# The opening in another order on four engines, and another place for T4's products, in a hybrid encoder kernel

## The chip, the core and the metric

The kernel runs on one core of one Trainium2 chip. The metric is the device time of one execution in microseconds (us), here as the median of several runs. The core's engines run side by side, each through a program of its own, in order: PE (TensorE: matrix products and transpositions; the load of its stationary operand is listed as PEld), DVE (VectorE), ACT (ScalarE) and POOL (GpSimd). SP (SyncE) issues most of the transfers. An engine that needs something of another waits for it, and everything behind it in its program waits as well.

## The reference

The input x of [1, 1024, 1024] float32, with 16 learned rows in front of it, runs through one layer. All is kept in float32 accuracy; the kernel gets it by splitting each float32 operand into a high and a low part and adding three products: high by high (hh), high by low (hl), low by high (lh).

```python
h = rmsnorm(h_res, norm1_w)                 # x * rsqrt(mean(x*x) + 1e-6) * w
proj = h @ w_in                             # q k v z beta a | sc_b sc_c sc_x | gate_a gate_b
o_dn = gated_deltanet_bidir(q, k, v, z, b_raw, a_raw, conv_w, A_log, dt_bias, dn_norm_w)
y_a = o_dn @ w_branch_dn
y_b = (sc_b * depthwise_conv_centred(sc_c * sc_x, sc_conv_w)) @ w_branch_sc
merged = sigmoid(gate_a) * y_a + sigmoid(gate_b) * y_b
h_res = h_res + merged @ w_out
h2 = rmsnorm(h_res, norm2_w)
gu = h2 @ w_gate_up
h_res = h_res + (silu(gu[..., :D_FF]) * gu[..., D_FF:]) @ w_down
out = rmsnorm(h_res, final_norm_w)[:, 16:]
```

## The kernel before

The program goes through stages: the opening (norm of nine row tiles of x, transposition, first products), the combined projection with the DeltaNet scans between its products, the merge gates, the two branch projections, the output projection, and the feed-forward part. In the opening and in the stage behind it, the order of PE, DVE and ACT is the order in which the code is written.

The opening works on tiles of 128 rows of h. Tile t is loaded into xs[t] (xr in the profile; tile 0 is the 16 learned rows and 112 rows of x). `square(t)` on ACT takes the sum of squares into ss and then its root; `normed(t)` on DVE takes a reciprocal, one Newton step on it (`inv_root`), and multiplies the tile by ss and by the row of norm weights, w1row. `turn(t, ...)` transposes the tile on PE by eight 128x128 transpositions into two PSUM banks, g = 0 for the first 512 columns and g = 1 for the rest. `high(t, g)` on ACT casts a bank into hTh (the high part), and `lows(t, g)` on DVE takes the low part (the tiles al). `weights(u)` splits the first weight tile of a unit u: ACT casts into wh, POOL subtracts into wl, each in two halves of four of the eight blocks k. `steps(gen0, KT, order)` then lets PE make the 24 products of a unit over 336 columns (bank pm, line 328), in an order of the three kinds hh, lh, hl. Behind them come the products `ba(0)` (lines 1125 and 1126), tile 3, and unit 1's products.

The norm weights reach all 128 partitions like this: w1one holds them as one row of 1024 on one partition, loaded third on SP's queue; PE multiplies a column of ones by it, 512 at a time, and DVE copies the two banks into w1row. `idle_turns(n)` makes n transpositions of the identity that nobody reads. The taps of the short convolutions are loaded as rows and turned by two transpositions, which ACT scales into wc and cols.

The loads of the opening are issued by SP in the order of the code. They take eight completion semaphores in turn, so the ninth load waits until the first has landed, and so on.

The last gate pair is made by `last_pair`. Its products are made by a scheme with seven block products instead of eight: A11 and so on are split weight tiles, B11, B12, B21 and B22 the four blocks of h transposed (tiles hTh and al), and S1 to S4 and T1 to T4 sums of blocks. `product(bank, a, b)` issues 12 products of 128x512 (line 1430). T4's product adds to the bank (pd) that holds S2 by T2 and S3 by T3. B11's product goes to a bank po (pe), ACT copies it to o1 (line 1598), and then B21's product adds to the same bank, so it must wait for that copy. Behind the pair the first branch projection starts (lines 134 to 136), over px: rows of p_d that ACT casts and DVE subtracts (lines 101 and 102) while the pair is made. This last part lies outside the stretches with a fixed order; a scheduler of the framework places its instructions on each engine.

## Time and profile before

| what | us |
|---|---|
| median of three runs | 1985.89 |
| lowest and highest of them | 1984.41, 1986.49 |
| the profiled execution, as a run | 1983.87 |
| its span, from the first to the last instruction | 1982.2 |
| PE busy within the span | 1966.1 |
| start of the first product of line 328 | 17.02 |
| start of the first product of line 134 | 1074.57 |

The prediction shows rows of several views. In the timeline and in the chain of waits a row begins with its start and its length in us from the start of the span; then come the engine, the line, the operation and the tiles, and in brackets how long the engine stood idle before it and what released it. A row of the waits gives the engine, what it waited for, the us in total, how often, and the longest. PE's rows in the timeline overlap: products are pipelined, and the length of one reaches to its modelled end, so the pace is read from the starts.

### The profile page before, as it was taken

Reading aid. Unit: us, or ns where it says so; the run is one execution under the profiler, and the core shown is the slowest. Engines: PE = TensorE matmul, PEld = TensorE weight load, DVE = VectorE, ACT = ScalarE, POOL = GpSimd, SP = SyncE. Lnnn points to the kernel's source line nnn. Section 1 sums busy time; section 2 is a strip of 40 time slices with the busy share of each in tenths; the row PEclk is TensorE's granted clock in tenths of the full one; section 3 lists DMA queues with packets and bytes.
Section 4 is the critical chain, followed back from the end, with each engine's and each line's share of the span. In section 5 each row is a group of like instructions: output and inputs, shape, how many; then the busy total and the mean of one; then the engine's idle time right before and its main releaser. Section 6 shows DMA issues by size and latency. Waiting matters only on the chain.

```text
span 1982.2 us, 31846 instructions
## 1 busy us (share of the span) xinstructions
PE 1966.1 (99%) x11999; PEld 1718.1 (87%) x11999; DVE 1396.6 (70%) x3015; ACT 839.1 (42%) x1968; POOL 107.7 (5%) x407
## 2 busy tenths in 40 slices
PE   9999999999999999999999999999999999999998
PEld 8999999999999999888888888888887888888887
DVE  6888688888888888844954544469676766646575
ACT  6472354636464646344444221225332333324344
POOL 2011101010101010100000000000000000000000
PEclk9999999999999999999999999999999999999999
DMA  3122222212122212222236743123366754477654
GB/s 134 66 90 75 61 86 60 76 60 76 59 76 60 76 59 76 70 86 95 97 128 240 247 157 99 64 85 111 123 224 235 250 186 167 170 274 245 192 172 169
DMA packets 124689, 251.52 MB, mean 127 GB/s; under 512 B 44981, under 2 KB 46438, under 8 KB 122103
## 3 DMA queue, kind: packets, MB, share of 16 engines
q1 hardware_dynamic: 123959, 248.44, 37.6%
q8 instruction: 94, 1.54, 0.3%
q10 hardware_dynamic: 576, 1.05, 0.1%
q14 instruction: 60, 0.49, 0.1%
HBM read 181.20 MB, written 68.25 MB: 126 GB/s over the span
## 4 chain that ended last, share of the span: by engine, by line
PE 92%; DVE 4%; DMA 3%; ACT 1%; issue 1%; SPq 0%; DVEq 0%; ACTq 0%
PE pm L328 31%; PE pd L1430 12%; PE pe L1430 6%; PE pm L1430 4%; PE pe L136 2%; PE pe L134 2%; PE pe L135 2%; PE pd L890 1%; PE pd L869 1%; PE pd L853 1%; PE pd L856 1%; PE pe L2040 1%; PE pe L2041 1%; PE pe L2039 1%; PE pd L886 1%; PE pe L590 1%
## 5 line engine op out<-in xcount | busy, mean ns | idle before, releaser
L328 PE MATMUL pm<-hTh,wh 128*128 128x320 f32 (+4 forms) x1248 | 428.4, 349 | 0.4 <-ACT hTh L1090 0.2
L328 PE MATMUL pm<-al,wh 128*128 128x320 f32 (+4 forms) x1248 | 427.7, 348 | 0.0
L328 PE MATMUL pm<-hTh,wl 128*128 128x320 f32 (+4 forms) x1248 | 425.9, 347 | 0.0
L328 PEld LDWEIGHTS pm<-hTh,wh 128*128 128x128 f32 x1248 | 233.9, 189 | 11.9 <-issue 1.3
L328 PEld LDWEIGHTS pm<-hTh,wl 128*128 128x128 f32 x1248 | 234.2, 189 | 10.2 <-issue 0.4
L328 PEld LDWEIGHTS pm<-al,wh 128*128 128x128 f32 x1248 | 234.1, 189 | 9.7
L102 DVE TENSOR_TENSOR al<-raw,ring_h 128x1024 fp32r<-128x1024 f32 x73 | 88.6, 1223 | 65.0 <-ACT ring_h L101 64.3
L101 ACT CAST ring_h<-raw 128x1024 fp32r<-128x1024 f32 x73 | 76.7, 1053 | 107.0 <-PE pd L2041 40.2
L350 DVE SCALAR_TENSOR_TENSOR kq<-ra,wc,kq 128x520 f32<-128x520 f32 x128 | 96.5, 754 | 4.9 <-ACT kq L380 4.0
L977 DVE TENSOR_TENSOR wl<-raw,wh 128x512 fp32r<-128x512 f32 x112 | 76.0, 689 | 31.1 <-ACT wh L980 30.4
L876 ACT ACTIVATE w<-pd,small 128x128 f32<-128x128 f32 x128 | 39.8, 363 | 125.0 <-PE pd L869 124.3
L487 DVE TENSOR_TENSOR fP<-fP,tm 128x135 f32<-128x135 f32 (+23 forms) x248 | 71.6, 289 | 5.1
L483 DVE TENSOR_TENSOR tm<-fP,fN 128x135 f32<-128x135 f32 (+23 forms) x248 | 71.8, 290 | 4.4
L980 ACT CAST wh<-raw 128x512 fp32r<-128x512 f32 x112 | 66.2, 621 | 3.7 <-issue 3.6
L101 ACT CAST wh<-raw 128x1024 fp32r<-128x1024 f32 x37 | 38.8, 1050 | 52.9 <-PE pm L135 16.6
L1978 ACT ACTIVATE b<-b 128x512 f32<-128x512 f32 x20 | 12.6, 632 | 103.6 <-DVE b L1396 103.6
L843 ACT ACTIVATE jk<-NP 128x128 f32<-128x128 f32 x64 | 19.9, 311 | 76.5 <-DVE NP L839 75.5
L102 DVE TENSOR_TENSOR wl<-raw,wh 128x1024 fp32r<-128x1024 f32 x37 | 45.1, 1220 | 10.0 <-ACT wh L101 9.9
L1430 PE MATMUL pd<-b_hl,wh 128*128 128x512 f32 x168 | 51.9, 390 | 0.0
L863 DVE SCALAR_TENSOR_TENSOR r<-pd,negEG,vS 128x128 f32<-128x128 f32 x120 | 36.7, 344 | 20.8 <-PE pd L853 20.4
L899 DVE SCALAR_TENSOR_TENSOR S<-S,eGl,pd 128x128 f32<-128x128 f32 x104 | 31.5, 340 | 28.1 <-PE pd L886 28.0
L1396 DVE TENSOR_TENSOR b<-pd,b 128x512 f32<-128x512 f32 x21 | 14.5, 689 | 51.9 <-PE pd L1430 51.9
(626 smaller groups left out, 4793.8 us busy)
## 6 DMA issues: line engine op xcount, KB each, us to landing
raw<-in_w_in_dram SPq DMA_DIRECT2D x72, 512.0 KB
raw<-in_w_gate_up_dram SPq DMA_DIRECT2D x44, 512.0 KB
sums<-in_w_down_dram SPq DMA_DIRECT2D x22, 512.0 KB
t_d<-sums SPq DMA_DIRECT2D x11, 1024.0 KB
raw<-s_d SPq DMA_DIRECT2D x44, 256.0 KB
raw<-t_d SPq DMA_DIRECT2D x44, 256.0 KB
act_d<-b SPq DMA_DIRECT2D x43, 256.0 KB
raw<-act_d SPq DMA_DIRECT2D x33, 256.0 KB
```

What stands on the lines that cost most here:

```text
L101: nc.scalar.copy(hi, src)
L102: nc.vector.tensor_tensor(out=lo, in0=src, in1=hi.bitcast(F32), op=ALU.subtract)
L134: mm(po[:m, :n], wh[:, k, :m], xhk[:, t0:t0 + n], start=(k == 0), stop=False)
L135: mm(po[:m, :n], wh[:, k, :m], xlk[:, t0:t0 + n], start=False, stop=False)
L328: mm(po[:, :n], ww[:, k], f(k)[:, t0:t0 + n], start=i == 0, stop=i == 3 * KT - 1)
L350: nc.vector.scalar_tensor_tensor(out=acc, in0=raw[:, h0 + t:h0 + t + hn], scalar=wc[:, t, col:col + 1], in1=acc, op0=ALU.mult, op1=ALU.add)
L483: nc.vector.tensor_tensor(out=tv, in0=fP[:, 0:r, j:j + 1].broadcast_to([P, r, n]), in1=fN[:, j:j + 1, j + 1:32].broadcast_to([P, r, n]), o ...
L487: nc.vector.tensor_tensor(out=fP[:, 0:r, j + 1:32], in0=fP[:, 0:r, j + 1:32], in1=tv, op=ALU.subtract)
L876: nc.scalar.activation(w[d], b2[:, 2 + d], AF.Copy, scale=ce[:, c, d:d + 1])
L977: nc.vector.tensor_tensor(out=u[1][1][:, k], in0=u[2][:, k], in1=u[1][0][:, k].bitcast(F32), op=ALU.subtract)
L980: nc.scalar.copy(u[1][0][:, k], u[2][:, k])
L1430: mm(po, x[:, k], at(y, k), start=i == 0 and not add_to, stop=i == 11, skip_group_check=add_to)
```

## The change

The norm weights come as eight rows of 128 (w1rows), by a load that ACT issues ahead of its table load. PE transposes them into eight columns (w1cols), DVE copies these, and PE transposes each column, broadcast to 128 columns, so that the bank holds the weights on all partitions; DVE copies the two banks into w1row as before. The idle turns become 8, 2, 12 and 2 instead of 8, 20, 4 and 4. The third tile is multiplied in two halves of 512 columns. The taps' transpositions move ahead of the third tile's and go into one bank. ACT casts the first half of the weights ahead of all transposed tiles, and then goes by halves of the columns: the first halves of the three tiles, with the second half of the weights between them, then the second halves. DVE takes the lows in the same order. A new tiny copy on POOL, from the last column of the third tile, writes into wl before the subtractions do. PE makes unit 0's hh and lh products of the first four blocks, then those of the other four, and then hl. In `last_pair`, T4's product moves behind B11's.

On PE the opening reads as follows, up to the first unit's products (pd, pe and pm are banks, ident the identity). First the program before, then the changed one:

```order
L98 MATMUL pd_185<-ident 128x128 x8
L1136 MATMUL pm_194<-w1one,ones_151 128x512
L1136 MATMUL pm_197<-w1one,ones_151 128x512
L98 MATMUL pd_227<-ident 128x128 x20
L98 MATMUL pe_248<-ident,xr_153 128x128 x4
L98 MATMUL pe_253<-ident,xr_153 128x128 x4
L98 MATMUL pd_264<-ident 128x128 x4
L98 MATMUL pd_269<-ident,xr_154 128x128 x4
```

```order
L98 MATMUL pd_184<-ident 128x128 x8
L98 MATMUL pm_193<-ident,w1rows 128x8
L98 MATMUL pd_196<-ident 128x128 x2
L98 MATMUL pm_199<-ident,w1cols 128x128 x4
L98 MATMUL pm_205<-ident,w1cols 128x128 x4
L98 MATMUL pd_239<-ident 128x128 x12
L98 MATMUL pe_252<-ident,xr_153 128x128 x4
L98 MATMUL pe_257<-ident,xr_153 128x128 x4
L98 MATMUL pd_262<-ident 128x128 x2
L98 MATMUL pd_265<-ident,xr_154 128x128 x4
```

The two products from w1one are gone, nine transpositions and two idle turns stand in their place, and the twenty idle turns ahead of the first tile have become twelve.

On ACT the stretch from the third tile's root to the last transposed tile reads as follows, before and changed (jk and ss belong to the squares, raw to the weights):

```order
L1070 ACTIVATE ss_218<-ss_218,eps 128x1
L1090 CAST hTh<-pe_248 128x4x128
L1090 CAST hTh<-pe_253 128x4x128
L1104 CAST wh_181<-raw_167 128x512 x2
L1090 CAST hTh<-pd_269 128x4x128
L1090 CAST hTh<-pd_274 128x4x128
L1090 CAST hTh<-pd_284 128x4x128
L1090 CAST hTh<-pe_289 128x4x128
```

```order
L1069 ACTIVATE ss_229<-ss_229,eps 128x1
L1105 CAST wh_180<-raw_166 128x512
L1091 CAST hTh<-pe_252 128x4x128
L1091 CAST hTh<-pd_265 128x4x128
L1105 CAST wh_180<-raw_166 128x512
L1091 CAST hTh<-pd_278 128x4x128
L1091 CAST hTh<-pe_257 128x4x128
L1091 CAST hTh<-pd_270 128x4x128
L1091 CAST hTh<-pe_283 128x4x128
```

The weights' first half has moved to the front, and the three first halves of the tiles (pe_252, pd_265, pd_278) stand ahead of the second ones.

On PE the last gate pair reads as follows around T4's products (pd from b and w), with B11's products ahead of them in the changed program; first before, then changed:

```order
L1430 MATMUL pm_12916<-b_2064_12135,mB_12908 128x512 x8
L1430 MATMUL pd_12915<-b_2108_12466,w_2087_12254 128x512 x12
L1430 MATMUL pe_12968<-hTh,wh_12898 128x512
L1430 MATMUL pe_12968<-al_124,wh_12898 128x512
L1430 MATMUL pe_12968<-hTh,wl_12899 128x512
```

```order
L1441 MATMUL pe_12953<-hTh,wh_12895 128x512
L1441 MATMUL pe_12953<-al_124,wh_12895 128x512
L1441 MATMUL pe_12953<-hTh,wl_12896 128x512
L1441 MATMUL pd_12912<-b_2108_12463,w_2087_12251 128x512 x12
L1441 MATMUL pe_12953<-hTh,wh_12895 128x512
L1441 MATMUL pe_12953<-al_125,wh_12895 128x512
L1441 MATMUL pe_12953<-hTh,wl_12896 128x512
```

T4's twelve products stand between B11's (hTh, al_124) and B21's (hTh, al_125). The scheduler also moved four of B22's products, which stood between B11's and B21's, behind them, and three additions of DVE ahead of pieces of px. Elsewhere the order on the engines is the same in both programs.

The diff, cut to its core:

```diff
@@ -322,7 +322,7 @@
         (wh, wl), (xh, xl) = w, xx
         t0 += C0
         parts = {"hh": (wh, lambda k: xh[:, k]), "hl": (wh, lambda k: xl[k]), "lh": (wl, lambda k: xh[:, k])}
-        seq = [(m, k) for m in sweep for k in range(KT)] if sweep else [(m, k) for k in range(KT) for m in ("hh", "hl", "lh")]
+        seq = [(m, k) for m, kk in sweep for k in kk] if sweep else [(m, k) for k in range(KT) for m in ("hh", "hl", "lh")]
         for i, (m, k) in enumerate(seq):
             ww, f = parts[m]
             mm(po[:, :n], ww[:, k], f(k)[:, t0:t0 + n], start=i == 0, stop=i == 3 * KT - 1)
@@ -1026,24 +1026,23 @@
         eps = st.tile([P, 1], F32, name="eps")
         nc.gpsimd.memset(warm, 1.0)
         nc.gpsimd.memset(eps, EPS)
-        nc.scalar.activation(warm, warm, AF.Sqrt)
         baT = d1.tile([P, L], F32, tag="vT", name="baT", bufs=2)[:64]
         wba = st.tile([P, KT, 64], F32R, name="wba")
         raw = st.tile([P, KT, 32], F32, name="wba_raw")
         rows = st.tile([P, 2, P], F32, name="rows")
         wc = c1.tile([P, 5, 24], F32, name="wc")
         size = lambda t: P if t < 8 else META
-        w1one = st.tile([1, D], F32, name="w1one")
-        ones1 = st.tile([1, P], F32, name="ones1")
-        nc.gpsimd.memset(ones1, 1.0)
-
+        w1rows = st.tile([KT, P], F32, name="w1rows")
+        w1cols = st.tile([P, KT], F32, name="w1cols")
+        nc.scalar.dma_start(w1rows, norm1_w.rearrange("o (k p) -> (o k) p", p=P))
+
+        nc.scalar.activation(warm, warm, AF.Sqrt)
         xs = [st.tile([P, D], F32, tag="xr", name=uid("xr"), bufs=9) for _ in range(9)]
         units = []
         for t, xr in enumerate(xs):
             if t == 0:
                 nc.sync.dma_start(xr[:META], meta)
                 nc.sync.dma_start(xr[META:P], x[0:P - META])
-                nc.sync.dma_start(w1one, norm1_w[0:1, :])
             else:
                 nc.sync.dma_start(xr[:size(t)], x[P * t - META:P * t - META + size(t)])
             if t == 2:
@@ -1069,18 +1068,20 @@
             nc.scalar.activation(jk[:p], xs[t][:p], AF.Square, accum_out=ss[:, 0:1])
             nc.scalar.activation(ss[:, 1:2], ss[:, 0:1], AF.Sqrt, scale=1.0 / D, bias=eps[:p])
 
-        def normed(t):
+        def normed(t, pieces=1):
 
             p, ss = size(t), scale[t]
             inv_root(ss)
-            nc.vector.scalar_tensor_tensor(out=xs[t][:p], in0=xs[t][:p], scalar=ss[:, 2:3], in1=w1row[:p],
-                                           op0=ALU.mult, op1=ALU.mult)
+            for i in range(pieces):
+                c = slice(D // pieces * i, D // pieces * (i + 1))
+                nc.vector.scalar_tensor_tensor(out=xs[t][:p, c], in0=xs[t][:p, c], scalar=ss[:, 2:3], in1=w1row[:p, c],
+                                               op0=ALU.mult, op1=ALU.mult)
 
         banks = {}
 
-        def turn(t, *make):
+        def turn(t, *make, gs=(0, 1)):
             p = size(t)
-            for g in range(2):
+            for g in gs:
                 pt = banks[t, g] = make[g]().rearrange("p (k t) -> p k t", k=4)
                 for k in range(4):
                     transpose(pt[:, k, :p], xs[t][:p, (4 * g + k) * P:(4 * g + k + 1) * P], p)
@@ -1097,9 +1098,9 @@
                 nc.vector.tensor_tensor(out=l_[:, :, c], in0=banks[t, g][:, k, :p],
                                         in1=hx[0][:, 4 * g + 2 * i:4 * g + 2 * i + l_.shape[1], c].bitcast(F32), op=ALU.subtract)
 
-        def weights(u):
-
-            for i in range(2):
+        def weights(u, parts=(0, 1)):
+
+            for i in parts:
                 k = slice(4 * i, 4 * i + 4)
                 nc.scalar.copy(u[1][0][:, k], u[2][:, k])
                 nc.gpsimd.tensor_tensor(out=u[1][1][:, k], in0=u[2][:, k], in1=u[1][0][:, k].bitcast(F32), op=ALU.subtract)
@@ -1128,37 +1129,47 @@
                     f()
             return lambda: nc.scalar.copy(baT[:, t0:t0 + n], po[:64, :n])
 
-        first, second = ("hh", "lh", "hl"), ("hh", "hl", "lh")
+        whole, halves = range(KT), (range(4), range(4, KT))
+        first, second = (tuple((m, whole) for m in ms) for ms in (("hh", "lh", "hl"), ("hh", "hl", "lh")))
+        opening = (*((m, kk) for kk in halves for m in ("hh", "lh")), ("hl", whole))
 
         idle_turns(8)
+        pw = psm()
+        transpose(pw[:, :KT], w1rows, KT)
+        nc.vector.tensor_copy(w1cols, pw[:, :KT])
+        idle_turns(2)
         for i in range(2):
             pw = psm()
-            mm(pw, ones1, w1one[:, 512 * i:512 * i + 512], start=True, stop=True)
+            for k in range(4):
+                transpose(pw[:, k * P:(k + 1) * P], w1cols[:, 4 * i + k:4 * i + k + 1].broadcast_to([P, P]))
             nc.vector.tensor_copy(w1row[:, 512 * i:512 * i + 512], pw)
         for t in range(3):
             square(t)
-            normed(t)
-        idle_turns(20)
+            normed(t, 1 + (t == 2))
+        idle_turns(12)
         turn(0, psd, psd)
+        idle_turns(2)
+        turn(1, pss, pss)
+        taps = psm()
+        transpose(taps[:, :120], rows[:120, 0], 120)
+        transpose(taps[:, 128:153], rows[:25, 1], 25)
+        turn(2, pss, psd, gs=(0,))
+        turn(2, pss, psd, gs=(1,))
+        nc.gpsimd.tensor_copy(u0[1][1][:, 0, 0:1], xs[2][:, D - 1:D])
+        weights(u0, (0,))
         high(0, 0)
-        high(0, 1)
-        weights(u0)
-        idle_turns(4)
-        turn(1, pss, pss)
-        idle_turns(4)
-        turn(2, pss, psd)
-        for t in (1, 2):
-            for g in range(2):
-                high(t, g)
-        for t, g in ((0, 0), (0, 1), (1, 0), (2, 0), (1, 1), (2, 1)):
-            lows(t, g)
-        pt0, pt1 = psd(), psd()
-        transpose(pt0[:, :120], rows[:120, 0], 120)
-        transpose(pt1[:, :25], rows[:25, 1], 25)
-        steps(gen0, KT, first)
-        nc.scalar.mul(wc.rearrange("p k t -> p (k t)"), pt0[:, :120], 0.5)
-        nc.scalar.copy(cols[:, :24], pt1[:, :24])
-        nc.scalar.mul(cols[:, 24:25], pt1[:, 24:25], 0.5)
+        high(1, 0)
+        weights(u0, (1,))
+        high(2, 0)
+        for t in range(3):
+            high(t, 1)
+        for g in range(2):
+            for t in range(3):
+                lows(t, g)
+        steps(gen0, KT, opening)
+        nc.scalar.mul(wc.rearrange("p k t -> p (k t)"), taps[:, :120], 0.5)
+        nc.scalar.copy(cols[:, :24], taps[:, 128:152])
+        nc.scalar.mul(cols[:, 24:25], taps[:, 152:153], 0.5)
         split(wba[:, :, 0:32], wba[:, :, 32:64], raw)
         evict = ba(0)
 
@@ -1592,10 +1603,10 @@
         nc.scalar.copy(o2[:, right], bank)
         product(bank2, A_["S1"], "T1")
         add(o2[:, right], bank2, o2[:, right])
-        product(bank, A_["A22"], "T4", True)
         po = psz()
         product(po, A_["A11"], "B11")
         nc.scalar.copy(o1[:, left], po)
+        product(bank, A_["A22"], "T4", True)
         add(o2[:, left], bank, o1[:, left])
         half_turn(o2[:, left])
         add(o2[:, right], o2[:, right], o1[:, left])
```

## The prediction

> **What bounds the kernel now.** I read the page first, then the waits of PE, then the chain of the opening, then the timeline of the two places that the diff touches. The page's first row says that PE works nearly always:
>
> ```profile
> PE 1966.1 (99%) x11999; PEld 1718.1 (87%) x11999; DVE 1396.6 (70%) x3015; ACT 839.1 (42%) x1968; POOL 107.7 (5%) x407
> ```
>
> So PE stands idle for 1982.2 - 1966.1 = 16.1 us, and only two things can shorten the run: PE work taken away, or PE's useless time (idle, or idle turns that only fill a wait). Of PE's waits these lie where the diff is:
>
> ```profile
> PE pm L1136 <- DMA w1one<-in_norm_w_dram: 1.7, 1, 1.7
> PE pd L98 <- POOL eps L2071: 1.6, 1, 1.6
> PE pe L1430 <- ACT s L1598: 0.7, 1, 0.7
> ```
>
> The chain of waits over the first 25 us (start, length, what) shows more useless time than the waits do, because idle turns count as work:
>
> ```profile
> 1.72 3.48 DMA w1one<-in_norm_w_dram
> 5.24 3.77 PE pm L1136 x4
> 9.02 3.91 PE pd L98 x20
> 13.80 1.76 PE pd L98 x16
> 15.61 0.66 PE pd L98 x4
> 17.02 4.00 PE pm L328 x24
> ```
>
> The first product of the model starts at 17.02. Behind it PE never waits more than fractions of a us, so what the opening gains there is gained at the end, if the next stages keep up.
>
> **The opening, part by part.** The rows of the timeline (start, length, engine, line):
>
> ```profile
> 0.81 1.28 ACT L1029 ACT_TABLE_LOAD   x1 [0.81 <-PEq L2116]
> 1.60 1.97 PE L98 MATMUL pd<-ident 128*128 128x128 f32 x8 [1.60 <-POOL eps L2071]
> 5.11 1.06 ACT L1069 ACTIVATE jk<-xr 128x1024 f32<-128x1024 f32 x1 [2.80 <-DMA xr<-in_x_dram]
> 6.35 0.29 ACT L1070 ACTIVATE ss<-ss,eps 128x1 f32<-128x1 f32 x1
> 8.82 1.06 ACT L1069 ACTIVATE jk<-xr 128x1024 f32<-128x1024 f32 x1 [0.60 <-DMA xr<-in_x_dram]
> 9.05 0.69 DVE L1137 COPY w1row<-pm 128x512 f32<-128x512 f32 x1 [1.01 <-PE pm L1136]
> 9.66 0.15 DVE L161 RECIPROCAL ss<-ss 128x1 f32<-128x1 f32 x1
> 10.00 0.30 ACT L1070 ACTIVATE ss<-ss,eps 128x1 f32<-128x1 f32 x1
> 10.35 1.28 DVE L1076 SCALAR_TENSOR_TENSOR xr<-xr,ss,w1row 128x1024 f32<-128x1024 f32 x1
> 11.55 0.15 DVE L161 RECIPROCAL ss<-ss 128x1 f32<-128x1 f32 x1
> 14.14 1.28 DVE L1076 SCALAR_TENSOR_TENSOR xr<-xr,ss,w1row 128x1024 f32<-128x1024 f32 x1
> 15.08 2.73 POOL L1105 TENSOR_TENSOR wl<-raw,wh 128x512 fp32r<-128x512 f32 x2 [13.49 <-DMA raw<-in_w_in_dram]
> 15.40 1.57 ACT L1090 CAST hTh<-pd 128x512 fp32r<-128x512 f32 x3
> 16.60 1.94 DVE L1097 TENSOR_TENSOR al<-pd,hTh 128x512 fp32r<-128x512 f32 x4
> 16.83 0.63 ACT L1090 CAST hTh<-pe 128x512 fp32r<-128x512 f32 x1
> 20.87 0.32 PE L1125 MATMUL pe<-hTh,wba 128*64 128x336 f32 x1
> 22.09 1.13 ACT L1104 CAST wh<-raw 128x512 fp32r<-128x512 f32 x2
> 24.12 1.49 PE L328 MATMUL pm<-hTh,wh 128*128 128x336 f32 x8
> ```
>
> At present the norm weights stand in w1row at 9.05 + 0.69 = 9.74, though the first tile's ss is ready at 6.64: DVE waits 3 us for the weights. From there it takes 1.89 us a tile (9.66 to 11.55) and ends the third at 15.42.
>
> First the weights. Two K=1 products (3.77 us of PE) go; a [8, 128] load, one transposition, a copy of 8 columns, eight transpositions and the same two copies come. The load moves from third on SP's queue to first on ACT's, at about 0.81; what is queued behind it there (table load, warm-up) ends 0.4 us later, at about 2.7, long before the first Square at 5.1. SP loses one issue, so its later loads start no later. How long this load takes is not in the trace; bounds come from the load above, 3.48 us behind 112 rows of x, and from a small lone load:
>
> ```profile
> 141.56 0.28 SPq L673 DMA_DIRECT2D mN<-ndm  x1
> 144.00 0.77 POOL L680 TENSOR_TENSOR tm<-mP,mN 1x15 f32<-1x15 f32 x1 [7.96 <-DMA mN<-ndm]
> ```
>
> That is 2.44 us, so it lands between 3.25 and 4.3; I take 3.5, nearer the first, since its queue is empty. PE's eight idle turns run until 3.57 anyway. A transposition with its tail and a copy of 8 columns take 0.42 + 0.15 (the L98 row further down, and DVE's one-column row above). Eight transpositions at 0.213, the slow pace of that L98 row, take 1.7 and a tail of 0.2; the first copy of w1row hides under the last four, the second takes 0.69. So w1row is ready at 3.57 + 0.57 + 1.9 + 0.69 = 6.75 (7.45 for the late landing). A broadcast source has no row; at best its weight loads cost what the others do, nothing beside the turns, at worst as much again, 1.7. I take the first, since only the addresses differ.
>
> Then DVE. Reciprocals come at 6.75, 8.64 and 10.53; the third tile's ss is ready at 10.30, as its Square waits for x, so little more is to be had here however early the weights come. The third multiply starts at 11.22 and now comes in halves, each about half of 1.28 plus a start: 11.97 and 12.6, against 15.42.
>
> Then the way to the first product. Half a tile's transpositions take 0.6 with their tail and the cast 0.63, so the last first-half cast ends at 12.15 + 0.6 + 0.6 = 13.35, and the first product starts at 13.4 instead of 17.02. It then runs in four groups: hh and lh of the first half, hh and lh of the second, four products each at 0.16 (24 from 17.02 to 20.87), and then the eight of hl. POOL's tiny copy holds its two subtractions back until the third multiply is done; at 2.73 for both, behind a handover of 0.2, they end near 14.2 and 15.6 (now 17.8). Three more casts at 1.57 for three end near 14.9. So PE waits 0.2 before the first lh and not quite 0.1 before the second, and hl starts at 16.35; DVE's lows (three of 512 and six of 256 columns, some 3.8 us by the 1.94 of two and two, from 12.5) end at 16.3, just in time. The ba products start at 17.65 instead of 20.87: 3.2 us. Bounds: 3.6 (no wait inside the 24 products) and 2.5 (load at 4.3). If POOL's cover of DVE's work were gone (its subtractions 0.5 later), lh would wait that 0.5 and hl with it.
>
> Late next is ACT. Its last cast of the three tiles ended at 17.46 and now ends near 14.9, 2.55 earlier, and the second unit's wh (22.09 + 1.13 = 23.22, used at 24.12) moves by that while PE moves by 3.2: its slack falls from 0.90 to 0.25. If that cover is gone, each tenth of ACT costs a tenth.
>
> **The last pair.** In T4's old place PE ran into ACT:
>
> ```profile
> 1062.62 2.88 PE L1430 MATMUL pd<-b,w 128*128 128x512 f32 x12
> 1068.27 1.05 ACT L101 CAST b<-mA 128x1024 fp32r<-128x1024 f32 x1 [1.37 <-DMA mA<-p_d]
> 1069.23 0.58 ACT L1598 COPY s<-pe 128x512 f32<-128x512 f32 x1
> 1069.86 0.51 PE L1430 MATMUL pe<-hTh,wh 128*128 128x512 f32 x1 [0.73 <-ACT s L1598]
> 1074.57 0.39 PE L134 MATMUL pe<-b,wh 128*128 128x512 f32 x1
> 1076.51 1.22 DVE L102 TENSOR_TENSOR b<-raw,b 128x1024 fp32r<-128x1024 f32 x1
> ```
>
> B21's products must wait until ACT has copied B11's, and the copy sits behind a cast. From T4's first product to the first one of the next stage PE takes 11.95 us for 48 products. A row of the chain gives twelve their undisturbed time:
>
> ```profile
> 1038.19 2.72 PE pm L1430 x12
> ```
>
> Four times 2.72 is 10.88, so 1.07 is lost (0.73 idle, the rest in the restart). With T4's 2.72 us between B11's and B21's, the copy runs at about 1065.6 and is done near 1066.2, 1.9 before PE wants it. What could be late next is the first dense product over px, whose last low piece DVE ends at 1077.73. The change puts three adds before the later pieces, but no new work; that piece is needed at 1073.5 + 7 x 0.68 + 0.23 = 1078.5. I take the full 1.07; bounds 0 and 1.07.
>
> **Sum.** 3.2 + 1.07 = 4.27 against the profiled execution's 1983.87: 1979.6. The runs shown lie 0.5 to 2.6 above that execution, their median 2.02. Part of this I lay on the clock of PE:
>
> ```profile
> L98 PE MATMUL pd<-ident x15: 394/421/475, 8.9 to 12.0; 128*128 128x128 f32 x15
> L98 PE MATMUL pe<-ident,xr x8: 272/273/273, 12.8 to 13.5; 128*128 128x128 f32 x8
> ```
>
> The same transposition takes 421 ns before about 12.2 us and 273 behind it (0.213 and 0.109 from one to the next): PE got its full clock 7 us after its unbroken work began at 5.24. If that comes later in another run, the 44 turns ahead of the third tile end 0.49 us later for each us, and at most, with all of them slow, some 2.6 later (28 turns at 0.104, less the slack of 0.3 in which PE waited for the third tile). I take 0.6, about the least by which a run shown lies above the profile. The changed opening keeps PE at work from 1.6 on, so its clock should rise by about 9, before anything on the path. Forecast for the median: 1985.89 - 4.27 - 0.6 = **1981.0**.
>
> **Rivals.** The load is late (ACT's queue shows nothing so early in this trace): landing at 5.2, as today's does, it makes w1row ready at 8.4 and moves the chain back by 1.65. That leaves 1.55 + 1.07, and half of the clock's 0.6: 1983.0. Against it, no large load is ahead of it.
> The last pair gives nothing, because its wait moves to px: 1981.0 + 1.07 = 1982.1. For it: DVE is full from 1065.64 to 1077.73. Against it: 0.8 us to spare.
> The clock stays low past the first product. The K=1 products and most idle turns go, and PE's turns now have gaps while DVE works. Then three tiles' turns run at 0.213 in line, the first product starts at 14.8 (1.4 lost), and each of the 336-column products takes twice its 0.16; if 7 us pass before the clock rises, as above, 3.5 more is lost. Together 4.9: 1985.89 - 4.27 + 4.9 = 1986.5, slower than before. It decides the sign once the clock is low for over 5.7 us behind the first product. Against it: in this trace the clock rose amid turns alone, with the last K=1 product 3.2 us past. The Trainium skill, "TensorE: Matmul & The Clock Gate", Part 4, says that transposes do not count as PE work for the gate, which would make this rival the rule; the trace disagrees, by the two L98 rows.
>
> **How the numbers follow.** Forecast 0.70 (own range 1979.2 to 1982.3: 3.6 with 2.0 of the clock, 2.5 with none), late load 0.10, last pair 0.10, clock 0.05, something unlisted 0.05. A measurement of this kernel can tell about 0.2% from no change, 4 us: faster means below 1981.9, close to the forecast. That takes 0.87 of the forecast, a fifth of the late load, 0.4 of the last pair: 0.67. Slower by as much needs something unlisted: 0.04. The rest, 0.29, lies within. The range 1979.0 to 1984.2 holds the forecast and two rivals.
>
> **What would show it.** First L328 product near 13.4 and first ba product near 17.65; w1row's second copy ending near 6.8; a wait of lh for POOL of 0.3; turns of 273 ns from about 9 on; no wait of B21's products for ACT, and 10.9 us from the start of B11's to the first dense product. I am wrong if w1row is ready after 8, if the L98 rows are at 421 past 11, if ACT's second wh makes PE wait near 21, or if the first dense products wait for DVE.

## The result, and the profile after

The changed kernel takes 1980.24 us (median of 11 runs, 1978.97 to 1983.87); the kernel before, run beside it, 1986.64 (11 runs, 1984.41 to 1988.70). The ratio is 0.9974, with an interval of 0.9966 to 0.9982: faster by 0.26%, 3.6 to 6.8 us. The forecast was 1981.0. The profiled execution took 1978.97, its span 1977.2 (1983.87 and 1982.2 before).

The page's row of busy time of the changed kernel:

```profile
PE 1961.2 (99%) x11992; PEld 1715.3 (87%) x11992; DVE 1395.8 (71%) x3017; ACT 838.5 (42%) x1968; POOL 106.6 (5%) x407
```

PE's idle time is what it was, 1977.2 - 1961.2 = 16.0 us; the 4.9 us came off its busy time. The prediction had this kind of gain in mind when it said that idle turns count as work. The waits of PE (engine, line, what it waited for: us in total, times, longest) have changed their names:

```profile
PE pe L98 <- DVE xr L1077: 2.3, 1, 2.3
PE pe L590 <- DVE PQ L629: 1.7, 2, 1.3
PE pd L739 <- issue: 1.6, 2, 1.0
PE pd L98 <- POOL ident masks.py:199: 1.5, 1, 1.5
PE pd L98 <- DVE ss L162: 0.7, 1, 0.7
```

The waits for w1one (1.7) and for ACT's copy in the last pair (0.7) are gone. In the opening PE now waits for DVE. New is 1.6 of "issue" at line 739, far from the edit; it has an experiment below.

The timeline of the opening (start, length, engine, line, and in brackets the idle time ahead of it):

```profile
3.40 0.27 PE L98 MATMUL pm<-ident,w1rows 8*128 8x8 f32 x1
4.08 1.62 PE L98 MATMUL pm<-ident,w1cols 128*128 128x128 f32 x8
5.18 1.29 DVE L1145 COPY w1row<-pm 128x512 f32<-128x512 f32 x2 [1.30 <-PE pm L98]
5.71 1.06 ACT L1068 ACTIVATE jk<-xr 128x1024 f32<-128x1024 f32 x1 [2.77 <-DMA xr<-in_x_dram]
7.28 0.16 DVE L161 RECIPROCAL ss<-ss 128x1 f32<-128x1 f32 x1 [0.81 <-ACT ss L1069]
11.77 1.41 DVE L1077 SCALAR_TENSOR_TENSOR xr<-xr,ss,w1row 128x512 f32<-128x512 f32 x2
13.52 2.55 POOL L1106 TENSOR_TENSOR wl<-raw,wh 128x512 fp32r<-128x512 f32 x2
13.93 0.88 PE L328 MATMUL pm<-hTh,wh 128*128 128x336 f32 x4
16.84 1.42 PE L328 MATMUL pm<-al,wh 128*128 128x336 f32 x8
18.09 0.32 PE L1126 MATMUL pe<-hTh,wba 128*64 128x336 f32 x1
19.96 1.13 ACT L1105 CAST wh<-raw 128x512 fp32r<-128x512 f32 x2
```

The weights stand in w1row at 5.18 + 1.29 = 6.47, earlier than the 6.75 of the forecast, but DVE then sat idle for 0.81: the first tile had landed at 5.6 (its Square starts at 5.71, 5.11 before), so its ss came at 7.25. The whole chain moved by that. ba starts at 18.09, 2.78 earlier than before; forecast was 3.2.

Of the last pair, T4's products, ACT's copy of B11's bank, and the first dense product (line 134):

```profile
1063.15 2.88 PE L1441 MATMUL pd<-b,w 128*128 128x512 f32 x12
1063.35 0.59 ACT L1608 COPY s<-pe 128x512 f32<-128x512 f32 x1
1071.31 0.39 PE L134 MATMUL pe<-b,wh 128*128 128x512 f32 x1
```

The copy is done at 1063.94, before B21's products by 1.9 us. B11's first product starts at 1060.43, so the 48 take 10.88, 11.95 before.

Subtracting the start of each matmul from that of its counterpart in the trace before shows where the 4.9 us come from: 2.78 by ba; down to 2.19 ahead of the last pair, since the issue waits are 1.0 longer than before (1.6 against 0.6) and smaller ones give 0.4 back; 3.26 behind the last pair; 4.61 behind 1510, where the trace before had a wait of 1.3 (line 1430 for DVE's b) that this one has not; 4.90 at the end. The rows of the trace before for these waits:

```profile
PE pd L1430 <- DVE b L1396: 1.3, 1, 1.3
PE pd L736 <- issue: 0.4, 1, 0.4
PE pd L739 <- issue: 0.2, 1, 0.2
```

### The profile page after: what moved, and what is told of

The parts are those of the page before. It is cut to its first block, busy times and chain, and to the rows that moved or that the text cites. A ratio compares the mean times of both kernels' runs of the same rounds, so it can differ in the third digit from the quotient of the medians.

```text
span 1977.2 us, 31834 instructions
## 1 busy us (share of the span) xinstructions
PE 1961.2 (99%) x11992; PEld 1715.3 (87%) x11992; DVE 1395.8 (71%) x3017; ACT 838.5 (42%) x1968; POOL 106.6 (5%) x407
## 4 chain that ended last, share of the span: by engine, by line
PE 92%; DVE 3%; DMA 2%; ACT 1%; issue 1%; SPq 0%; POOL 0%; DVEq 0%; POOLq 0%; ACTq 0%
PE pm L328 30%; PE pd L1441 14%; PE pe L1441 7%; PE pm L1441 5%; PE pe L136 2%; PE pe L135 2%; PE pe L134 2%; PE pd L869 1%; PE pd L890 1%; PE pd L853 1%; PE pe L2051 1%; PE pe L2052 1%; PE pe L2050 1%; PE pd L856 1%; PE pe L590 1%; PE pd L886 1%
```

## Experiments

Each kernel was timed in five rounds beside the kernel before. A ratio's interval is about 0.1% to each side, 2 us, so for single parts the traces decide: "behind the first reciprocal" counts from the start of DVE's first RECIPROCAL, which takes the landing of the first tile out of the comparison.

### The last pair alone, and the opening alone

To the kernel before, only this:

```diff
-        product(bank, A_["A22"], "T4", True)
         po = psz()
         product(po, A_["A11"], "B11")
         nc.scalar.copy(o1[:, left], po)
+        product(bank, A_["A22"], "T4", True)
```

> The kernel before with T4's products moved between B11's and B21's, nothing else. Theory (the prediction's last-pair term): B21's products no longer wait for ACT's copy, 48 products take 10.9 us from the first of B11 to the first dense product (line 134), 11.95 before, and the time falls by 1.07: 0.05%, ratio 0.9995, which times alone can hardly tell, so the profile decides. Rival: the wait moves to the first dense products over px (DVE is full there), so that between the start of the pair and the end of the first dense bank nothing is gained: 0.

Measured: 1983.2 (1980.38 to 1987.28, 11 runs), ratio 0.9990 (0.9981 to 0.9999). In the trace the 48 products take 10.88 from 1063.68 to 1074.56. The gain is kept: the matmuls of the next stages run on without a wait for px. But the opening of this run, the old one without any edit, came out 0.92 later than in the trace before (ba at 21.79). The timeline shows why; the turns are slow for longer:

```profile
8.91 4.53 PE L98 MATMUL pd<-ident 128*128 128x128 f32 x20
13.23 1.50 PE L98 MATMUL pe<-ident,xr 128*128 128x128 f32 x8
```

The same 20 turns took 3.98 in the trace before, and the first tile's eight 1.04. The record of the granted clock rises to full at 14.16 here, at 12.22 there.

The changed kernel with the same lines put back in their old order:

```diff
-        po = psz()
-        product(po, A_["A11"], "B11")
-        nc.scalar.copy(o1[:, left], po)
         product(bank, A_["A22"], "T4", True)
+        po = psz()
+        product(po, A_["A11"], "B11")
+        nc.scalar.copy(o1[:, left], po)
```

> The changed kernel with the last pair put back in its old order, so the opening alone. Theory (opening and pair are separate terms, the rest of the 5 us seen between the two profiled executions is chance in places that the change does not touch): ba's first product near 18.1 as in the changed kernel (20.87 before), B21's wait for ACT back at 0.7, time below before by 2.8: ratio 0.9986. Rival (the earlier opening also shifts the later stages into a better place, so that 4 us or more come from it): ratio 0.998 or less, with ba's first product still at 18.1.

Measured: 1979.39 (1978.48 to 1980.87, 6 runs), ratio 0.9969 (0.9956 to 0.9981). ba at 17.80, and the pair takes 11.61, of which PE waits 0.44 for ACT. By the times the opening alone does as much as the whole change, which the rival said; the trace does not give it 6 us. Against the trace before, 3.07 is gained by ba and 2.97 left at the pair; the pair gives 0.34 (old order both times, but a shorter wait), and 1.6 comes at 1510. The last two owe nothing to the opening as far as the traces show. Where the rest of the difference of the medians is from is taken up below.

### Which part of the opening: the weights or the order

The kernel before with the new weights only (load on ACT's queue, w1one, ones1 and the K=1 products gone):

```diff
-            mm(pw, ones1, w1one[:, 512 * i:512 * i + 512], start=True, stop=True)
+            for k in range(4):
+                transpose(pw[:, k * P:(k + 1) * P], w1cols[:, 4 * i + k:4 * i + k + 1].broadcast_to([P, P]))
```

> The kernel before with the norm weights loaded first on ACT's queue and spread by transpositions; the order of everything else is the old one. Theory (DVE's chain of three tiles sets the opening, and the weights held up its start): reciprocals near 7.3, 9.2 and 11.1, third multiply whole and done near 13.1 (15.42 before), first L328 product near 14.6, first ba product near 18.5: a gain of 2.3 of the 2.8. Rival (the order of the casts, halves and products on ACT and PE gives the gain, early weights alone end in a wait elsewhere, for POOL's wl or ACT's casts): ba after 20, gain below 0.9.

Measured: 1984.31 (1981.02 to 1986.37, 11 runs), ratio 0.9988 (0.9979 to 0.9996). Reciprocals at 6.90, 8.80 and 10.69, each 0.4 ahead of the theory's and in its steps, but ba at 19.01, not 18.5: 1.86 gained, 12.11 behind the first reciprocal where the changed kernel needs 10.81. The timeline shows the missing part, POOL and DVE in the same stretch:

```profile
11.30 3.49 POOL L1104 TENSOR_TENSOR wl<-raw,wh 128x512 fp32r<-128x512 f32 x2 [9.85 <-ACT wh L1103]
11.38 2.27 DVE L1075 SCALAR_TENSOR_TENSOR xr<-xr,ss,w1row 128x1024 f32<-128x1024 f32 x1
```

The third multiply takes 2.27 instead of 1.28, POOL's pair 3.49 instead of 2.55. Early weights bring POOL's subtractions onto the multiply that everything waits for.

The new order alone: the changed opening with the old load and the K=1 products, 20 idle turns and the old pair.

```diff
-        nc.scalar.dma_start(w1rows, norm1_w.rearrange("o (k p) -> (o k) p", p=P))
+                nc.sync.dma_start(w1one, norm1_w[0:1, :])
...
-        idle_turns(12)
+        idle_turns(20)
```

> The changed kernel's order on the four engines (third multiply in halves, casts and products by halves, POOL's small copy, taps early) with the weights by the old load and K=1 products, 20 idle turns, and the last pair in its old order. Theory: w1row is ready at 9.7 as before, the third multiply's halves end near 14.9 and 15.5, first L328 product near 16.2, first ba product near 20.1: a gain of 0.5 to 0.9. Rival (the order carries the gain): ba before 19, gain near 2.

Measured: 1983.42 (1981.52 to 1986.67, 11 runs), ratio 0.9986 (0.9977 to 0.9995), yet ba at 20.89 against 20.87: the order alone gains nothing in the opening (0.16 when counted from the first reciprocal, 11.04 against 11.20). The first product comes at 16.84, not 16.2: w1one landed 0.2 later than in the trace before (5.44 and 5.24), and the 20 turns were slow (4.19 us, clock up at 12.85) and kept the first tile's turns until 13.17. So neither part holds the whole gain: the weights alone give 1.86 of 2.78 and need the order, which keeps POOL away, for the rest, and the order needs the weights. It also shows how little a ratio says of a part this small: 2.5 us by the medians, none at the place of the edit.

### POOL's copy, and the halves

```diff
-        nc.gpsimd.tensor_copy(u0[1][1][:, 0, 0:1], xs[2][:, D - 1:D])
```

> The changed kernel without POOL's copy of one column, so that POOL's two subtractions may run while DVE multiplies the second and third tile. Theory of the change (POOL's work slows DVE's beside it): the third multiply's halves end later than 13.2 by 0.3 to 1.0, and the first L328 product with them, though lh no longer waits for wl: ba 0 to 0.7 later. Rival (the copy only holds wl back): halves end at 13.2 as before, PE's wait of 0.33 ahead of the first lh goes, ba near 17.8: 0.3 better.

Measured: 1981.42 (1979.82 to 1983.76, 8 runs), ratio 0.9976 (0.9965 to 0.9986). ba comes 11.97 behind the first reciprocal, 1.16 later than in the changed kernel; the theory had the sign and half the size. Its timeline:

```profile
10.48 1.48 POOL L1106 TENSOR_TENSOR wl<-raw,wh 128x512 fp32r<-128x512 f32 x1 [9.03 <-ACT wh L1105]
10.99 0.98 DVE L167 SCALAR_TENSOR_TENSOR ss<-ss 128x1 f32<-128x1 f32 x1
12.21 2.43 DVE L1077 SCALAR_TENSOR_TENSOR xr<-xr,ss,w1row 128x512 f32<-128x512 f32 x2
12.83 1.26 POOL L1106 TENSOR_TENSOR wl<-raw,wh 128x512 fp32r<-128x512 f32 x1 [0.87 <-ACT wh L1105]
```

Even a step on one column, 0.22 elsewhere, lasts 0.98 beside POOL, and the halves 2.43 instead of 1.41. The ends of these rows say more: the step on one column ends at 10.99 + 0.98 = 11.97, and POOL's first subtraction at 10.48 + 1.48 = 11.96. So DVE seems to stand until POOL's instruction is over, rather than to run slowly beside it. DVE's lows, which read a bank and one tile, ran at their usual 0.68 and 0.64 beside POOL in the changed kernel. The Trainium skill, "GPSIMD Engine Reference", Key points, has it so: POOL and VectorE share the way to SBUF and collide where VectorE has two SBUF inputs; these rows agree.

The third multiply whole instead of in halves:

```diff
-            normed(t, 1 + (t == 2))
+            normed(t)
```

> The changed kernel with the third multiply in one piece instead of two halves. Theory of the change (the first half of the third tile reaches PE and ACT earlier): the multiply ends 5.1 us after DVE's first reciprocal starts, where the first half ended at 5.2 less 0.7, so the first L328 product comes 0.5 later (7.2 us behind the first reciprocal, 6.65 with halves), but its followers wait less for POOL, and ba comes 0.1 to 0.5 later (11.3 behind the first reciprocal, 10.8 with halves). Rival (POOL's wl, which starts behind the whole tile in both, sets the end): ba 10.7 to 10.8 behind the first reciprocal, nothing lost.

Measured: 1980.71 (1979.01 to 1982.22, 9 runs), ratio 0.9973 (0.9963 to 0.9983). First product 7.22 and ba 11.29 behind the first reciprocal: the halves are worth 0.48 at ba, the upper end of what was expected.

### Why the first tile was late

```diff
                 nc.sync.dma_start(xr[META:P], x[0:P - META])
+                nc.sync.dma_start(rows[:120, 0], dn_conv_w[0].rearrange("k (t p) -> (k t) p", p=P))
...
-                nc.sync.dma_start(rows[:120, 0], dn_conv_w[0].rearrange("k (t p) -> (k t) p", p=P))
```

> The changed kernel with the small load of rows moved on SP's queue from behind x2 and raw0 to between x0 and x1, so that x1 is issued 0.6 us later. Theory (x0 lands at 5.6 in the changed kernel and at 5.0 before because x1's load, issued 0.4 earlier there, shares the way with it; DVE's chain starts with x0): first Square at 5.1, reciprocals at 6.7, 8.6 and 10.4, first L328 product near 13.4, ba near 17.5: 0.5 to 0.6 below the changed kernel. Rival (x0 is late for the weights' load on ACT's queue or by chance): first Square stays at 5.5 to 5.7, ba at 18.1, or later if x2 now holds the third tile up.

Measured: 1980.43 (1979.4 to 1981.04, 5 runs), ratio 0.9967 (0.9955 to 0.9980). The first Square starts at 5.19, but the second only at 8.13 (7.16 in the changed kernel), so the second reciprocal waits 0.89 for it and ba comes at 18.54, 0.45 later. Nor does x1's load explain the late first tile: in the nine traces with the changed kernel's loads the first Square starts between 5.16 and 5.86, in the four with the old loads between 5.06 and 5.35. Some 0.3 of the 0.6 may be the order; the rest varies from run to run.

### What raises PE's clock

All 24 idle turns of the opening taken out:

```diff
-        idle_turns(8)
...
-        idle_turns(2)
...
-        idle_turns(12)
...
-        idle_turns(2)
```

> The changed kernel without the idle turns ahead of the first tile (the 8 and the 2 around the transposition of w1rows, the 12 ahead of the first tile, the 2 behind it). Theory (PE's clock rises at the end of the first window of 3.41 us, on a grid of its own, that is full of turns or products; idle turns are what fills it early): the clock rises only behind the first L328 products, near 16 to 19, the three tiles' turns take 421 ns each, first L328 product near 14.4, the products until the rise take twice as long, ba near 20 to 21.5: 2 to 3.5 us slower than the changed kernel. Rival (DVE's chain sets the pace and the turns that lie between are enough): ba at 18.1 to 18.6, 0 to 0.5 slower.

Measured: 1979.59 (1978.57 to 1980.62, 5 runs), ratio 0.9965 (0.9952 to 0.9977). The clock rises at 12.62, ba comes at 18.62, 0.53 later than in the changed kernel and 0.42 when counted from the first reciprocal. The theory's slow products did not come: two tiles' turns, the first of them at the slow pace from 9.43 on, were enough to bring the clock up. Nor do the times show a loss, as the median lies 0.6 below the changed kernel's: its trace has no issue wait, which makes up for most of what it loses in the opening and near 289 (both below). And the trace shows when the weights land, as nothing covers it:

```profile
2.70 0.24 PE L98 MATMUL pm<-ident,w1rows 8*128 8x8 f32 x1 [2.70 <-DMA w1rows<-in_norm_w_dram]
```

Then the idle turns replaced by K=1 products of 512 columns of ones:

```diff
-        idle_turns(8)
+        k1_turns(2)
...
-        idle_turns(2)
...
-        idle_turns(12)
+        k1_turns(4)
...
-        idle_turns(2)
```

> The changed kernel with its idle turns replaced by K=1 products of 128x512 of a row of ones (2 for the first 8 turns, 4 for the 12), so that PE is busy as long but with one row of the array; the 2 turns around the first tile are left out. Theory (K=1 products keep PE busy and do not raise its clock, as the three traces with the old weights suggest: 12.2, 12.8 and 14.2, always the end of the first window that held turns alone): as without idle turns, the clock rises behind the first L328 products, 2 to 3.5 us slower than the changed kernel. Rival (any unbroken work raises the clock, and the old kernel's gap until 5.2 is what made it late): clock up before 9, ba near 18.1, no loss.

Measured: 1986.01 (1984.47 to 1990.76, 11 runs), ratio 0.9996 (0.9987 to 1.0005). Each such product turned out to be two instructions of 0.9, so the four last until 14.75 and hold the first tile's turns back by 5 us; the time answers nothing about the clock. The clock does:

```profile
1.59 3.78 PE L1120 MATMUL pd<-ones 1*128 1x512 f32 x4 [1.59 <-POOL ones L1030]
7.56 7.19 PE L1120 MATMUL pd<-ones 1*128 1x512 f32 x8
14.68 1.97 PE L98 MATMUL pe<-ident,xr 128*128 128x128 f32 x8
```

PE is busy from 1.59 on but for 0.3 us, and the clock is full only at 19.10: products with one row of the array keep PE busy and do not raise it.

### The issue waits at line 739

Counting matmuls from the start of the program, the waits of PE behind the opening that nothing explains come at the same positions in every trace that has them, within two (3778, 6319, 6954), amid a burst of 32x32 products (once of 64x64), whichever product stands there. The changed kernel, with 7 matmuls fewer ahead of the model, waits 1.0 at the 3778th; the kernel before passes it without a wait. So here is the kernel before with 7 idle turns fewer:

```diff
-        idle_turns(20)
+        idle_turns(13)
```

> The kernel before with 13 idle turns instead of 20 behind the K=1 products, so that PE's program has as many instructions ahead of the model as the changed kernel (11992 products and turns in all). Theory (PE's 'issue' waits at lines 736 and 739 come at fixed positions of its program, about the 3778th and the 6953rd matmul in every trace so far, and last long where such a position falls into a burst of small products): a wait of 0.8 to 1.0 appears at the 3778th matmul, near 493, which the kernel before has not, 1.4 to 1.6 in all (0.6 before); the opening keeps its end or gains up to 1, since the turns were in the way while the clock was low. Rival (these waits are chance, or belong to the changed opening): 0.2 to 0.9 in all, as in the two traces with 11999.

Measured: 1984.15 (1981.63 to 1986.66, 11 runs), ratio 0.9988 (0.9980 to 0.9997). The waits of its PE:

```profile
PE pd L739 <- issue: 1.2, 2, 0.8
```

0.8 of it stands at the 3777th matmul. So this wait hangs on the count of instructions ahead and not on what the opening does; that the total is 1.2 and not 1.4 is the second wait, 0.4 here at the 6953rd. The other half of the expectation failed: ba came at 22.09, 1.2 later than before. With the turns gone ACT's casts came earlier, POOL started at 14.39, beside the third multiply, which took 2.36: the same collision as above.

### First halves first, and no idle turns to count

DVE multiplies the first halves of the second and third tile ahead of both second halves; turns, casts and products follow.

```diff
-        opening = (*((m, kk) for kk in halves for m in ("hh", "lh")), ("hl", whole))
+        lo_, hi_ = halves
+        opening = (("hh", lo_), ("hh", hi_), ("lh", lo_), ("hl", lo_), ("lh", hi_), ("hl", hi_))
...
-            normed(t, 1 + (t == 2))
+            inv_root(scale[t]) if t else normed(0)
+            if t:
+                scaled(t, 0)
+        for t in (1, 2):
+            scaled(t, 1)
```

> The changed kernel with DVE's order changed: the first halves of the second and third tile are multiplied ahead of both second halves; turns and casts follow that order, and the first unit's products go hh, hh, lh and hl of the first half, then lh and hl of the second. Theory (DVE's first halves set the first product, POOL's wl only the two lh groups): first L328 product 0.6 earlier (6.0 behind the first reciprocal's start, 6.65 in the changed kernel), ba 0.4 earlier (10.4 behind the first reciprocal, 10.8 in the changed kernel); issue waits of 1.2 to 1.6 as in the changed kernel, whose count of instructions it has. Rival (POOL's wl or DVE's lows end last whatever the order): ba 10.8 or later behind the first reciprocal.

Measured: 1980.28 (1979.13 to 1982.13, 7 runs), ratio 0.9972 (0.9961 to 0.9983). First product 6.49 and ba 10.62 behind the first reciprocal: 0.16 and 0.19 gained, not 0.6 and 0.4. The trace shows what the expectation left out: in PE's program the turns of the second halves stand ahead of the first product, and the last of them start at 12.81, when DVE is done with all halves (10.68 + 2.08 = 12.76). The issue waits are there (1.2), as its count of instructions demands.

The same with the idle turns replaced by two products of 512 columns with all rows, which makes the program 20 matmuls shorter:

```diff
-        idle_turns(8)
+        full_products(1)
...
-        idle_turns(2)
...
-        idle_turns(12)
+        full_products(1)
...
-        idle_turns(2)
```

> The order of the run with first halves first, and the 24 idle turns replaced by two products of the identity with 512 columns of ones, so that PE's program is shorter by 20 instructions pairs (11972 in all, near the 11968 of the run without turns, which had no issue wait). Theory (issue waits hang on the position in PE's program; products with all 128 rows raise the clock as turns do): issue waits of lines 736 and 739 fall to 0 to 0.3 (1.6 in the changed kernel), the clock rises before 9.5, ba as in the run with first halves first, and the end comes 1.5 to 2 earlier than in the changed kernel: near 1978.5. Rival (the waits are chance, or the gaps left by the turns keep the clock low): issue waits above 0.8, or the rise after 11 and ba 0.5 or more later.

Measured: 1977.68 (1976.96 to 1979.55, 5 runs), ratio 0.9960 (0.9948 to 0.9972): the fastest of all here, 8.8 us below the kernel before in the same runs (1986.49). There is no issue wait in its trace, and the clock rises at 8.48. The span is 1977.0 all the same, as one new loss stands in it. The windows of the trace show it (stretch and its length, busy time of PE, PEld, DVE, ACT and POOL with counts, granted clock, DMA), first of this run, then of the changed kernel:

```profile
285.00:288.30 3.30, 1.64 (x16) 1.30 (x8) 3.19 (x10) 1.59 (x6) 0.42 (x2) 1.00 0.49 159
288.40:291.70 3.30, 3.30 (x104) 2.83 (x103) 3.23 (x9) 0.58 (x2) 0.00 (x0) 0.50 0.02 5
```

```profile
285.20:288.50 3.30, 1.98 (x28) 1.35 (x17) 3.21 (x10) 1.88 (x6) 0.42 (x2) 1.00 0.44 152
288.60:292.00 3.40, 3.40 (x111) 3.26 (x104) 3.30 (x9) 0.36 (x1) 0.00 (x0) 1.00 0.02 5
```

PE waits 1.66 there for DVE (line 590, 1.33 in the changed kernel), its busy time in that stretch falls from 1.98 to 1.64, and it gets half its clock for the next 3.4 us; compared matmul by matmul, this run falls back by 1.2 between 287.7 and 290.5. The run without turns shows the same at 289. Why the wait is longer in these two stays open, and so does what exactly costs the clock: in the changed kernel's opening PE was busy for 1.71 of the 3.3 us from 5.3 to 8.6, hardly more, and kept its full clock.

## Why the prediction was right, step by step

**Opening, 3.2 forecast, 2.78 measured.** The mechanism held: without early weights the gain is nothing, and from the first reciprocal to ba the forecast had 17.65 - 6.75 = 10.9 and the trace 10.81. (Its terms 3.57 + 0.57 + 1.9 + 0.69 make 6.73, not 6.75, which changes nothing.) The step that was mis-sized is "Reciprocals come at 6.75", which took the first tile's ss as ready at 6.64 as in the trace before. It came at 7.25, 0.53 later for DVE, by a landing that varies by 0.7 between traces.

**The load, taken as 3.5 of 3.25 to 4.3.** Both bounds were too late: in the run without turns it had landed by 2.70. In the changed kernel the idle turns hid that. The broadcast source cost nothing beside the turns: without idle turns its eight transpositions took 1.97 at the slow pace, as the first eight idle turns do.

**Third multiply in halves, POOL's cover.** Right; worth 0.48 and 1.16. The prediction let the copy hold POOL's subtractions back, but priced only a later lh, at 0.5, and did not name what the copy keeps away: subtractions that run into the multiply, which then takes nearly twice as long.

**ACT late next.** The forecast slack of 0.25 was met exactly: wh at 19.96 + 1.13 = 21.09, u1's first product at 21.34. PE did not wait for it.

**Last pair, 1.07.** Met in the profiled pair, and 10.88 in all nine traces of the new order. The five traces of the old order take 11.95, 11.61, 12.12, 11.26 and 11.45, so the gain is 0.4 to 1.2 by the run, 0.8 on average; the forecast's 1.07 came from one of them. The rival of px is out, as no trace of the new order has a wait there.

**Clock, 0.6.** Right in kind: the old opening pays for a late rise, and 1.94 us later cost 0.92, 0.47 for each, where 0.49 was forecast. In the six traces with the changed opening's idle turns it rises at 5.26 to 7.65, always ahead of the first tile's turns. The reason given was wrong, though ("7 us after its unbroken work began", so a rise at about 9): K=1 products did not count. The traces fit windows of 3.413 us on a grid of its own: in the trace before the clock is full from 12.22 to 1978.30, 576 such windows, and in all fourteen traces the times between changes of the clock are whole numbers of them. The Trainium skill, "TensorE: Matmul & The Clock Gate", Part 1, describes free-running windows of 3413 ns; the traces agree. In thirteen traces the clock rises at the end of the first window that products or turns over all rows nearly fill (with 2.9 of its 3.41 us in the least, where 13 idle turns are left in the kernel before). The fastest kernel is the exception: PE was busy for 3.15 us of its window from 1.65 to 5.07, which brought no rise, and for 2.74 of the next, which did. So the share that is needed stays open. On such a grid the old opening's rise should fall between about 12 and 15.5, by the phase, an estimate; the four traces with the old weights have 12.13 to 14.16. At 0.47 for each us that would lose 0 to 1.6 against the trace before; the changed opening's rise does not matter. The rival by Part 4 of that page, that transposes do not count, is out for the transpositions of this kernel: in the changed kernel, nothing but turns raised the clock at 5.26.

**Not foreseen.** The issue waits took 1.0 back between 490 and 870, and the trace before carried a chance wait of 1.3 at 1510 (the same wait lies between 0 and 2.1 in the other traces) that the sum knew nothing of. The two nearly cancel, and beside the kernel before the time fell by 6.4 where the forecast had 4.9 (1985.89 - 1981.0), so part of the closeness of 1981.0 to 1980.24 is luck.

**What stays open.** The traces tie 2.78 + 0.8 (pair) + 0.8 (clock, half of 1.6, an estimate) - 1.0 = 3.4 us to the edits; the medians differ by 6.4, the interval begins at 3.6. So up to half of the measured gain has no place in the traces. The kernel before itself looks like the odd one: its profiled execution lies 2.6 below the median of its runs (1983.87 and 1986.5), while those of the other thirteen kernels lie between 1.3 below and 1.5 above theirs. And four edited kernels measure some 2 to 4 us better against it than their traces explain: the order alone (2.5, nothing gained at ba), 13 turns (2.3, with ba 1.2 later), the last pair alone (2.7 for 1.07) and the K=1 products (0.3, with ba 3.4 later). So the build before seems to lose 2 to 3 us in most runs at a place that its one trace does not show; without a second trace of it that is argued, not shown.

## What to carry to other kernels

An early operand on the critical chain is worth only what the next resource lets through: here early weights alone gave 1.86 of 2.78, and the rest needed an order that kept POOL's two-input work away from DVE's, so look for what a faster step will run into before counting it. Work that fills a wait should fill it for a reason that the trace shows: here turns over all rows raised PE's clock, and one-row products did not. And when an edit changes the number of instructions ahead of a burst of very short ones, look for waits far behind it that have no cause in the data flow.

## What the runs showed that was not expected

PE stalls without a releaser at fixed positions of its program: 0.5 to 1.0 us near the 3778th matmul in all nine traces of kernels with 11980 to 11993 matmuls, none over 0.15 there in the five with 11968, 11972, 11999 (two) and 12006. The Trainium skill, "Runtime: NRT & Kernel Launch", Instruction fetch mechanics, says that an engine streams its program in blocks of 256 instructions, which is mostly hidden; a fetch that falls behind in a burst of products 16 ns apart would fit, but no run here shows the fetch itself. And PE's clock fell by half for one window of 3.41 us when a single wait left it busy for 1.64 of 3.3 us (two traces). With 1.98 at the same place it did not, nor with 1.71 in the opening, so the busy time alone does not settle it.
